# A transformer block with expert retrieval on one core: two more run-ahead chunks of the first expert product, issued earlier, and a reduction in place of four additions

## The chip, the core and the metric

The kernel runs on one core of a Trainium2 chip. The core has five engines with a queue each: PE (matrix products, into the PSUM memory), DVE and POOL (elementwise work), ACT (activations, copies, and here the evacuation of PSUM), and SP, which here only issues DMA transfers. Each queue is worked off in order: an instruction that waits holds up everything behind it on its engine. The metric is the device time of one execution in microseconds. Before the change it was 1732.71 us, the median of three executions (1732.04 to 1734.6).

## What is computed

Input and output are 512 tokens of 1024 numbers, float32. The first sub-layer mixes tokens (two kinds of attention, gates, an output projection, residual add). The change lies behind it, in the second sub-layer, a retrieval over 16384 single-neuron experts:

```python
q = (xb @ w_q).reshape(PEER_BLOCK, PEER_HEADS, 2, PEER_HALF)
scores = jnp.einsum('thpd,hpkd->thpk', q, sub_keys).astype(jnp.float32)
top_s, top_i = lax.top_k(scores, PEER_TOPK)
...
best_s, best_pos = lax.top_k(cand_s, PEER_TOPK)
expert = jnp.take_along_axis(cand_i, best_pos, axis=-1)
gate = jax.nn.softmax(best_s, axis=-1)
act = jax.nn.gelu(jnp.einsum('thkd,td->thk', u[expert], xb).astype(jnp.float32),
                  approximate=False)
return jnp.einsum('thk,thkd->td', (gate * act).astype(v.dtype), v[expert])
```

Each token has 8 heads with 16 experts each; an expert is a pair of keys (a, b), each of 128.

## The kernel before

The tokens are worked on in four tiles of 128. For one tile (GT, tile 0) the experts' rows of u and v are gathered by indirect DMA, and DVE forms dot products and weighted sums. For the other three (DT, 384 tokens) the kernel works densely: it computes u·x for all 16384 experts in 128 chunks of 128, applies Gelu, multiplies by a sparse matrix of gates, and multiplies by v.

*A chunk of the first product* is `first` (line 678): a 512 KB load of *ut* (two buffers, issued by SP); a split into a high part *uh* on ACT (line 673) and the remainder *ul* on POOL (line 674), in two halves with three buffers each; 24 matmuls into *pa* (lines 148 to 150, two PSUM buffers); and Gelu on ACT into *ga* (line 687), which has AHEAD buffers, so that chunks can run ahead.

*The decoding of the keys* is `retrieve` (line 638), once for each tile and each half of the key. ACT broadcasts the selector into a one-hot tile *oh* (line 646, two buffers), DVE compares it (line 647), multiplies it with the indices (line 649) and sums over the last axis of 16 (lines 651 to 653). The result is *ia* or *ib*. Behind the last tile's, DVE forms the row numbers *ex* (line 658), on which the gathers on POOL (line 762) wait. Between its steps `more(n)` issues chunks.

*The expansion* (lines 715 to 754): for each of the three dense tiles the keys are transposed on PE (line 718), copied by ACT (*sel*, line 720), and in eight blocks of 16 tokens DVE builds one-hots and weights (*o1*, *o2*, *ow*, lines 738 to 742: five ops of 2048 elements), PE multiplies them (*pg*, line 747, 32 matmuls), ACT evacuates the gates into *gres* (the first 8 chunks') and *stage*, and SP writes *stage* to *spool* in DRAM. One chunk is issued in each block, and behind the last block what AHEAD still lacks.

*The main loop* (line 799) has 128 iterations. Iteration i2 loads *vt*, splits it into *vh* (ACT) and *vl* (DVE), multiplies *ga* by *gres* (line 810) or by a slice of *gs*, read back from *spool* (line 813), splits that into *wh* and *wl*, issues chunk i2 + AHEAD, and accumulates 18 matmuls into *acc*. Behind each group of matmuls `tick` moves the gathered tile on by its pace (PACE): gathers on POOL, dot products (line 774) and weighted sums (line 784) on DVE.

What stands in an engine's queue is not the order of the text: a scheduler moves instructions of one engine past each other, so that chunks of the main loop appear among the expansion's blocks. The order of each queue is fixed when the kernel is built.

Of the kernel before, what the change touches and what calls it, by code (L numbers as in the profile page):

```python
# [15 lines left out]
OP = mybir.AluOpType  # L16
AX = mybir.AxisListType
# [13 lines left out]
OCT = 8  # L31
TB = 16
TI = 4
AHEAD = 37
S2, GAT, WB, UB, VB = 8, 4, 3, 3, 3
COLS = 3 * 3 * D
PACE = 1.05 * 2 * P * len(GT) / (COLS * (2 * P - AHEAD))

# [9 lines left out]
def block_kernel(ctx, tc, x, mix_gain, w_in, gate_bias, q_gain, k_gain, sinks, w_up_a, w_up_b, w_out,  # L48
                 ffn_gain, w_q, keys_t, peer_u, peer_v, peer_ut, out):
    nc = tc.nc  # L50
    V, A, G = nc.vector, nc.scalar, nc.gpsimd
# [93 lines left out]
    def mm3(ps, l, r, li, ri, start, stop):  # L145

        bg.tick(ps.shape[1] * 3)
        nc.tensor.matmul(ps, lhsT=l[0][li], rhs=r[0][ri], start=start, stop=False)  # L148
        nc.tensor.matmul(ps, lhsT=l[0][li], rhs=r[1][ri], start=False, stop=False)  # L149
        nc.tensor.matmul(ps, lhsT=l[1][li], rhs=r[0][ri], start=False, stop=stop)  # L150
# [487 lines left out]
    def retrieve(j):  # L638

        r = NT - 1 - j  # L640
        ia, ib = (gwk.tile([P, HEADS, 16], F32, name=f"{n}{j}") if j in DT else
                  rp.tile([P, HEADS, 16], F32, name=f"{n}{j}") for n in ("ia", "ib"))
        for sel, half, dst in ((a_, 0, ia), (b_, 1, ib)):
            oh = rp.tile([P, HEADS, 16, 16], BF16, name="oh", tag="oh", bufs=2)
            oh2 = oh.rearrange("p h k j -> p (h k) j")
            A.activation(oh2, sel[:, r, :, None].to_broadcast([P, P, 16]), AF.Copy)
            V.tensor_tensor(out=oh2, in0=oh2, in1=i16[:, None, :].to_broadcast([P, P, 16]), op=OP.is_equal)
            yield
            V.tensor_tensor(out=oh, in0=oh, in1=idf[:, r, :, half, None, :].to_broadcast([P, HEADS, 16, 16]), op=OP.mult)
            yield  # L650
            for n in (8, 4, 2):
                V.tensor_tensor(out=oh[:, :, :, 0:n], in0=oh[:, :, :, 0:n], in1=oh[:, :, :, n:2 * n], op=OP.add)  # L652
            V.tensor_tensor(out=dst, in0=oh[:, :, :, 0], in1=oh[:, :, :, 1], op=OP.add)
            yield
        KEYS[j] = ia, ib, gate[:, r]
        if j in GT:
            ROWS[j] = gwk.tile([P, HEADS, 16], I32, name=f"ex{j}")
            V.scalar_tensor_tensor(out=ROWS[j], in0=ib, scalar=128.0, in1=ia, op0=OP.mult, op1=OP.add)
# [19 lines left out]
    def first(i2):  # L678

        ut = us.tile([P, KD, P], F32, name="ut", tag="ut", bufs=2)  # L680
        nc.sync.dma_start(ut, peer_ut[i2])
        u = split(us, ut, "u", G, UB)
        pa = pa_.tile([P, 512], F32, name="pa", tag="pa")
        for k in range(KD):
            mm3(pa[:, :T], u[k // 4], h2T, (SL, k % 4, SL), (SL, k, slice(0, T)), k == 0, k == KD - 1)
        ga = upool.tile([P, T], F32, name="ga", tag="ga", bufs=AHEAD)
        A.activation(ga, pa[:, :T], AF.Gelu)  # L687
        return ga
# [3 lines left out]
    def more(n):  # L692
        for i2 in range(len(ahead), min(len(ahead) + n, AHEAD)):
            ahead[i2] = first(i2)

    more(2)
    for j in DT + GT:
        for i, _ in enumerate(retrieve(j)):
            if i % 3 == 0:
                more(1)  # L700
    ret.close()

# [1 line left out]
    with ExitStack() as st:  # L704
# [4 lines left out]
        oh = [P, TB // TI, P, TI]  # L709
# [5 lines left out]
        for j in DT:  # L715
# [15 lines left out]
            for tb in range(P // TB):  # L731
# [11 lines left out]
                for q in range(TB // TI):  # L743
                    pp = pg.tile([P, TI, P], F32, name="pg", tag="pg")
                    for i in range(TI):
                        for s in range(2):
# [7 lines left out]
                                  stage.rearrange("p (o i) t -> p o i t", i=OCT))  # L754
    more(AHEAD)

# [42 lines left out]
    for i2 in range(P):  # L799
# [15 lines left out]
        V.tensor_tensor(out=wl, in0=ga, in1=wh.bitcast(F32), op=OP.subtract)  # L815
        if i2 + AHEAD < P:
            ahead[i2 + AHEAD] = first(i2 + AHEAD)
        for b in range(2):
# [46 lines left out]
```

## Time and profile before

| | |
|---|---|
| median of 3 executions | 1732.71 us (1732.04 to 1734.6) |
| the profiled execution, its own time | 1733.96 us |
| its span, first to last instruction | 1732.2 us |
| PE busy | 1658.3 us (96%) |
| PE weight loads busy | 1470.5 us (85%) |
| DVE busy | 1329.1 us (77%) |
| POOL busy | 811.8 us (47%) |
| ACT busy | 746.2 us (43%) |
| DMA, mean | 209 GB/s |

The profile's picture of 40 slices, 43.3 us each, has a digit for each engine's busy tenths (9 is 90% or more) and one for the granted clock of TensorE. PE has a 9 in most slices; slices 13 and 14 (6 and 7, 520 to 606 us) are low, and in the first of them the clock row has its only digit under 9. This is the decoding of the keys; the expansion follows to about 801 us, then the main loop to the end. Elapsed time follows PE from 905 us on. A line of a timeline or of the chain gives the start in us, a duration in us, the engine, the line of code and the tiles written and read; "x8" merges eight instructions, and brackets hold the idle time in front and what ended it.

### The profile page before, as it was taken

The page shows a single profiled execution, that of the slowest core. Times are in us where ns is not written, and L with a number is a line of the kernel's source. Part 1 is how long each engine was busy: PE and PEld are TensorE (multiplying, and loading weights), DVE is VectorE, ACT ScalarE, POOL GpSimd, SP SyncE. Part 2 cuts the span into 40 slices and gives each one's busy share as a digit, 9 for nine tenths or more (in the row PEclk, how much of TensorE's full clock was granted, in tenths as well). Part 3 has the DMA queues.
Part 4 walks back from the last instruction along what each step waited for, and adds up shares of the span by engine and source line. Part 5 has one row for each costly group of instructions (what it writes and reads, how often), then busy time and mean ns, then how long its engine had stood idle before and what let it go on. Part 6 is the DMA issues. An engine that isn't in the chain of part 4 may idle for free.

```text
span 1732.2 us, 24914 instructions
## 1 busy us (share of the span) xinstructions
PE 1658.3 (96%) x8969; PEld 1470.5 (85%) x8969; DVE 1329.1 (77%) x2289; ACT 746.2 (43%) x1457; POOL 811.8 (47%) x628
## 2 busy tenths in 40 slices
PE   6999999999996799989899999999999999999998
PEld 5987777798885798989789999999999999998886
DVE  5444345736999998898999888898887878877874
ACT  4457635533324454545233443443343434343443
POOL 4100011512323644455567767776776666763310
PEclk9999999999998999999999999999999999999999
DMA  4321221133301365757998988989889888887874
GB/s 154 97 79 50 73 96 50 61 97 120 101 9 56 113 194 153 210 162 263 363 342 324 331 278 322 317 289 327 302 287 326 308 300 306 290 279 237 290 238 146
DMA packets 158347, 361.30 MB, mean 209 GB/s; under 512 B 10384, under 2 KB 86160, under 8 KB 156304
## 3 DMA queue, kind: packets, MB, share of 16 engines
q1 hardware_dynamic: 120496, 224.94, 38.7%
q0 software_dynamic: 36864, 134.23, 22.3%
q8 instruction: 70, 1.15, 0.3%
q10 hardware_dynamic: 864, 0.54, 0.1%
q14 instruction: 53, 0.43, 0.1%
HBM read 331.89 MB, written 27.26 MB: 207 GB/s over the span
## 4 chain that ended last, share of the span: by engine, by line
PE 78%; DVE 14%; issue 4%; POOL 2%; ACT 1%; DMA 1%; DVEq 0%; POOLq 0%; ACTq 0%
PE acc L148 10%; PE acc L150 10%; PE acc L149 10%; PE pa L150 8%; PE pa L148 8%; PE pa L149 8%; PE pg L747 5%; PE mm L149 5%; PE mm L150 5%; PE mm L148 5%; DVE tt L566 1%; PE z L462 1%; DVE oh L652 1%; PE mm L490 1%; DVE idx L568 1%
## 5 line engine op out<-in xcount | busy, mean ns | idle before, releaser
L674 POOL TENSOR_TENSOR ul<-ut,uh 128x512 fp32r<-128x512 f32 x256 | 388.4, 1519 | 183.4 <-ACT uh L673 172.7
L148 PE MATMUL pa<-h2Th,uh 128*128 128x384 f32 x1024 | 349.9, 342 | 16.8 <-ACT uh L673 16.4
L150 PE MATMUL pa<-h2Th,ul 128*128 128x384 f32 x1024 | 350.5, 342 | 9.0 <-POOL ul L674 9.0
L149 PE MATMUL pa<-h2Tl,uh 128*128 128x384 f32 x1024 | 348.8, 341 | 0.0
L149 PE MATMUL acc<-vl,wh 128*128 128x512 f32 x768 | 300.3, 391 | 4.6 <-DVE vl L674 4.6
L673 ACT ACTIVATE uh<-ut 128x512 fp32r<-128x512 f32 x256 | 160.8, 631 | 332.6 <-PE pa L149 234.3
L674 DVE TENSOR_TENSOR vl<-vt,vh 128x512 fp32r<-128x512 f32 x256 | 257.6, 1007 | 58.5 <-ACT vh L673 57.6
L148 PE MATMUL acc<-vh,wh 128*128 128x512 f32 x768 | 301.9, 393 | 0.0
L150 PE MATMUL acc<-vh,wl 128*128 128x512 f32 x768 | 300.7, 392 | 0.0
L762 POOL DMA_INDIRECT row<-peer_v,ex x128 | 157.5, 1231 | 162.9 <-DVE xg L784 120.4
L762 POOL DMA_INDIRECT row<-peer_u,ex x128 | 162.9, 1272 | 124.8 <-PE pa L150 51.2
L673 ACT ACTIVATE vh<-vt 128x512 fp32r<-128x512 f32 x256 | 159.8, 624 | 131.2 <-PE acc L150 128.9
L148 PEld LDWEIGHTS pa<-h2Th,uh 128*128 128x128 f32 x1024 | 196.1, 192 | 22.3 <-ACT uh L673 17.8
L150 PEld LDWEIGHTS pa<-h2Th,ul 128*128 128x128 f32 x1024 | 195.8, 191 | 11.9 <-POOL ul L674 11.9
L149 PEld LDWEIGHTS pa<-h2Tl,uh 128*128 128x128 f32 x1024 | 195.8, 191 | 3.7
L784 DVE SCALAR_TENSOR_TENSOR xg<-row,wt,xg 128x1024 f32<-128x1024 f32 x128 | 185.9, 1453 | 1.4 <-DMA row<-peer_v,ex 0.7
L774 DVE SCALAR_TENSOR_TENSOR row<-row,h 128x1024 f32<-128x1024 f32 x128 | 178.5, 1406 | 3.9 <-DMA row<-peer_u,ex 3.8
L149 PEld LDWEIGHTS acc<-vl,wh 128*128 128x128 f32 x768 | 144.7, 188 | 34.2 <-DVE vl L674 6.8
L150 PEld LDWEIGHTS acc<-vh,wl 128*128 128x128 f32 x768 | 144.6, 188 | 32.3
L148 PEld LDWEIGHTS acc<-vh,wh 128*128 128x128 f32 x768 | 144.5, 188 | 26.4
L158 DVE TENSOR_TENSOR wlo<-w,whi 128x1024 fp32r<-128x1024 f32 x52 | 65.0, 1251 | 87.1 <-ACT whi L157 82.9
L813 DVE TENSOR_TENSOR ga<-ga,gs 128x384 f32<-128x384 f32 x120 | 93.9, 798 | 44.3 <-ACT ga L687 44.3
(231 smaller groups left out, 2775.7 us busy)
## 6 DMA issues: line engine op xcount, KB each, us to landing
ut<-peer_ut SPq DMA_DIRECT2D x128, 512.0 KB
vt<-peer_v SPq DMA_DIRECT2D x128, 512.0 KB
spool<-stage SPq DMA_DIRECT2D x24, 960.0 KB
gs<-spool SPq DMA_DIRECT2D x15, 1536.0 KB
w<-w_in SPq DMA_DIRECT2D x17, 1024.0 KB
w<-w_q SPq DMA_DIRECT2D x8, 1024.0 KB
w<-w_out SPq DMA_DIRECT2D x4, 1024.0 KB
x<-x SPq DMA_DIRECT2D x4, 512.0 KB
```

Of the source, the lines that this page charges most:

```text
L148: nc.tensor.matmul(ps, lhsT=l[0][li], rhs=r[0][ri], start=start, stop=False)
L149: nc.tensor.matmul(ps, lhsT=l[0][li], rhs=r[1][ri], start=False, stop=False)
L150: nc.tensor.matmul(ps, lhsT=l[1][li], rhs=r[0][ri], start=False, stop=stop)
L158: eng.tensor_tensor(out=lo, in0=raw, in1=hi.bitcast(F32), op=OP.subtract))
L462: nc.tensor.matmul(z[:, :nk], lhsT=qT[:, h, cols(NT - 1 - j)], rhs=kbT[:, h // 2, row0(j):S], start=True, stop=True)
L673: A.activation(hi, src[:, 4 * b:4 * b + 4], AF.Copy)
L674: eng.tensor_tensor(out=lo, in0=src[:, 4 * b:4 * b + 4], in1=hi.bitcast(F32), op=OP.subtract)
L747: nc.tensor.matmul(pp[:, i, :], lhsT=o1[:, q, :, i], rhs=ow[:, s, q, :, i], start=(s == 0), stop=(s == 1))
L762: G.indirect_dma_start(out=t, out_offset=None, in_=src, in_offset=bass.IndirectOffsetOnAxis(ap=ex[:, h, k:k + 1], axis=0))
L774: V.scalar_tensor_tensor(out=t, in0=t, scalar=1.0, in1=h2, op0=OP.mult, op1=OP.mult, accum_out=wt[:, h, k:k + 1]))
L784: V.scalar_tensor_tensor(out=xj, in0=t, scalar=wt[:, h, k:k + 1], in1=xj, op0=OP.mult, op1=OP.add))
L813: V.tensor_tensor(out=g3, in0=g3, in1=gs[:, :, (i2 - RES) % OCT, :], op=OP.mult)
```

## The change

Three edits. AHEAD, the number of chunks that may run ahead of the main loop, goes from 37 to 39 (two more *ga* buffers, and PACE, which depends on it, rises by 219/217). In front of the decoding 8 chunks are issued instead of 2, and during it one at every second step instead of every third; a tile has 6 steps before and after, so 3 instead of 2. The text thus issues 8 + 12 = 20 chunks by the end of the decoding instead of 2 + 8 = 10; the expansion still issues one in a block, until AHEAD is reached. And each of the eight sums over 16 is one tensor_reduce, whose result is float32 as before, instead of additions of 8, 4, 2 and 1 pairs in 16-bit numbers. The lines behind the sum have numbers lower by 2 in the changed kernel.

```diff
-AHEAD = 37
+AHEAD = 39
...
-            for n in (8, 4, 2):
-                V.tensor_tensor(out=oh[:, :, :, 0:n], in0=oh[:, :, :, 0:n], in1=oh[:, :, :, n:2 * n], op=OP.add)
-            V.tensor_tensor(out=dst, in0=oh[:, :, :, 0], in1=oh[:, :, :, 1], op=OP.add)
+            V.tensor_reduce(out=dst, in_=oh, axis=AX.X, op=OP.add)
...
-    more(2)
+    more(8)
     for j in DT + GT:
         for i, _ in enumerate(retrieve(j)):
-            if i % 3 == 0:
+            if i % 2 == 0:
                 more(1)
```

How the queues change is seen at three places. The first is DVE's queue at the start of the decoding, for the first tile's two halves; *idf* holds the indices, *i* the numbers 0 to 15. Before:

```order
L647 TENSOR_TENSOR oh<-oh,i_3676 128x2048
L649 TENSOR_TENSOR oh<-oh,idf 128x2048
L652 TENSOR_TENSOR oh<-oh 128x128x8
L652 TENSOR_TENSOR oh<-oh 128x128x4
L647 TENSOR_TENSOR oh<-oh,i_3676 128x2048
L652 TENSOR_TENSOR oh<-oh 128x128x2
L649 TENSOR_TENSOR oh<-oh,idf 128x2048
L653 TENSOR_TENSOR ia_5144<-oh 128x128
```

In the changed kernel:

```order
L647 TENSOR_TENSOR oh<-oh,i_3676 128x2048
L649 TENSOR_TENSOR oh<-oh,idf 128x2048
L651 TENSOR_REDUCE ia_5366<-oh 128x128
L647 TENSOR_TENSOR oh<-oh,i_3676 128x2048
L649 TENSOR_TENSOR oh<-oh,idf 128x2048
L647 TENSOR_TENSOR oh<-oh,i_3676 128x2048
L651 TENSOR_REDUCE ib_5367<-oh 128x128
```

Each half has three DVE ops instead of six, and the third is the sum.

The second place is ACT's queue from the last one-hot broadcast of the decoding to the first evacuation of the expansion. Before:

```order
L646 ACTIVATE oh<-b__5053 128x2048
L673 ACTIVATE uh<-ut 128x512
L687 ACTIVATE ga<-pa 128x384
L673 ACTIVATE uh<-ut 128x512 x3
L687 ACTIVATE ga<-pa 128x384
L673 ACTIVATE uh<-ut 128x512
L720 ACTIVATE sel<-pg 128x256
L673 ACTIVATE uh<-ut 128x512 x2
L687 ACTIVATE ga<-pa 128x384
L673 ACTIVATE uh<-ut 128x512 x2
L687 ACTIVATE ga<-pa 128x384
L750 ACTIVATE gres<-pg 128x8x4
```

In the changed kernel:

```order
L646 ACTIVATE oh<-b__5053 128x2048
L671 ACTIVATE uh<-ut 128x512 x2
L685 ACTIVATE ga<-pa 128x384
...
L685 ACTIVATE ga<-pa 128x384
L718 ACTIVATE sel<-pg 128x256
L671 ACTIVATE uh<-ut 128x512 x2
L685 ACTIVATE ga<-pa 128x384
L671 ACTIVATE uh<-ut 128x512 x2
L685 ACTIVATE ga<-pa 128x384
L748 ACTIVATE gres<-pg 128x8x4
```

Between the last broadcast and *sel* stood two finished chunks (*ga*); now there are nine. On PE the key transposes stand behind chunk 19, and 22 chunks and three matmuls stand ahead of the first block's products; before there were 13 chunks and six matmuls.

The third place is PE's queue from the last block's products to the first accumulation (*acc*). Before, the rest of chunk 34 and the chunks 35, 36 and 37 stand between them:

```order
L747 MATMUL pg_7703<-ow_7664,o1_7662 128x128
L149 MATMUL pa_7764<-h2Tl_3170,uh_7760 128x384
...
L150 MATMUL pa_7902<-h2Th_3169,ul_7899 128x384
L148 MATMUL acc1_7871<-vh_7879,wh_7887 128x512
L149 MATMUL acc1_7871<-vl_7880,wh_7887 128x512
L150 MATMUL acc1_7871<-vh_7879,wl_7888 128x512
```

In the changed kernel:

```order
L745 MATMUL pg_7901<-ow_7862,o1_7860 128x128
L148 MATMUL pa_8105<-h2Th_3169,uh_8097 128x384
...
L148 MATMUL acc1_7921<-vh_7929,wh_7937 128x512
L148 MATMUL acc2_7922<-vh_7929,wh_7937 128x512
L148 MATMUL acc3_7923<-vh_7929,wh_7937 128x512
L149 MATMUL pa_8105<-h2Tl_3170,uh_8097 128x384
L150 MATMUL pa_8105<-h2Th_3169,ul_8098 128x384
L148 MATMUL pa_8105<-h2Th_3169,uh_8097 128x384
L149 MATMUL acc1_7921<-vl_7930,wh_7937 128x512
```

Here `pa_8105` is chunk 41, of which seven matmuls stand between the last block and the first accumulation; the chunks 39 and 40 stand among the first blocks of the third tile, and the last four blocks follow each other with no chunk between them.

## Rows read from the trace of the kernel before

**Rows 1.** Windows: us, busy us (instructions) of five engines, granted PE clock, DMA share, GB/s.

```profile
542.00:546.00 4.00, 3.54 (x12) 3.04 (x11) 3.93 (x6) 3.97 (x4) 0.00 (x0) 0.52 0.27 100
815.00:905.00 90.00, 83.68 (x406) 73.30 (x406) 87.74 (x117) 30.73 (x60) 57.53 (x45) 0.98 0.94 360
905.00:1600.00 695.00, 695.00 (x3506) 630.80 (x3505) 578.59 (x657) 277.36 (x508) 480.59 (x366) 1.00 0.87 301
```

**Rows 2.** Waits of PE, 505 to 610 us: total us, times, longest us.

```profile
PE pa L148 <- ACT uh L673: 16.4, 4, 10.2
PE pa L150 <- POOL ul L674: 7.3, 6, 1.5
PE pg L747 <- DVE o L742: 4.6, 1, 4.6
```

**Rows 3.** Timeline of PE: the fourth matmul of chunk 4.

```profile
545.63 0.46 PE L148 MATMUL pa<-h2Th,uh 128*128 128x384 f32 x1
```

**Rows 4.** Timelines of ACT and DVE at the start of the second token tile's expansion.

```profile
664.41 0.39 ACT L720 ACTIVATE sel<-pg 128x256 f16<-128x256 f32 x1
666.85 4.55 DVE L740 TENSOR_TENSOR ow<-o,part 128x2048 f16<-128x2048 f16 x2
679.16 1.22 DVE L741 TENSOR_TENSOR o<-rep,sel 128x2048 bf16<-128x2048 f16 x1
684.84 1.21 DVE L741 TENSOR_TENSOR o<-rep,sel 128x2048 bf16<-128x2048 f16 x1
```

**Rows 5.** Chain: products of each token tile's first block, and the last block.

```profile
608.00 3.96 PE pg L747 x32
...
677.02 3.96 PE pg L747 x32
...
746.69 3.93 PE pg L747 x32
...
797.64 3.82 PE pg L747 x32
```

**Rows 6.** Groups of DVE by form, 543 to 596 us: busy us, mean ns | idle.

```profile
L652 DVE TENSOR_TENSOR oh<-oh 128x1024 bf16<-128x1024 bf16 x8 | 9.8, 1223 | 0.0
...
L652 DVE TENSOR_TENSOR oh<-oh 128x512 bf16<-128x512 bf16 x8 | 6.9, 868 | 0.1
L652 DVE TENSOR_TENSOR oh<-oh 128x256 bf16<-128x256 bf16 x8 | 6.8, 849 | 0.0
L653 DVE TENSOR_TENSOR ia<-oh 128x128 f32<-128x128 bf16 x4 | 2.8, 704 | 0.0
```

**Rows 7.** Timeline of DVE and POOL beside two subtractions on POOL.

```profile
480.03 2.38 POOL L158 TENSOR_TENSOR wlo<-w,whi 128x1024 fp32r<-128x1024 f32 x1 [4.10 <-ACT whi L157]
...
480.97 0.29 DVE L567 MAX8 vals<-tt 128x8 f32<-128x128 f32 x1
...
486.53 2.39 POOL L158 TENSOR_TENSOR wlo<-w,whi 128x1024 fp32r<-128x1024 f32 x1 [4.12 <-ACT whi L157]
486.70 2.30 DVE L574 TENSOR_TENSOR cs<-vals 128x64 f32<-128x64 f32 x1
```

**Rows 8.** Groups of DVE by form, whole span: two reductions.

```profile
L193 DVE TENSOR_REDUCE qass<-s 128x8 f32<-128x512 f32 x4 | 2.7, 682 | 2.6 <-ACT s L191 2.6
...
L193 DVE TENSOR_REDUCE kass<-s 128x4 f32<-128x256 f32 x2 | 0.8, 415 | 0.4 <-ACT s L191 0.4
```

**Rows 9.** Chain: first matmuls of a chunk, an accumulation, the next chunk.

```profile
895.28 0.17 PE pa L148
...
899.45 0.24 PE acc L148
...
903.57 0.17 PE pa L148
```

**Rows 10.** Timelines of DVE and PE at the loop's entry.

```profile
801.72 7.14 DVE L810 TENSOR_TENSOR ga<-ga,gres 128x384 f32<-128x384 f32 x8 [5.39 <-ACT gres L750]
...
814.65 0.39 PE L148 MATMUL acc<-vh,wh 128*128 128x512 f32 x1
```

## The prediction

> **What bounds the kernel now.** I read the windows first. From 905 to 1600 us PE, the matmul engine, is busy in all 695 us [rows 1]: there every microsecond is PE's work, and the work is the same in both kernels (128 chunks of the first product, 128 accumulations, 24 blocks of expansion). So the change can only move the time in which PE stands still or runs at the low clock, all of it between 513 and 905 us. The list of waits gives the stills of the decoding stage: 10.2 us on ACT's *uh* (an Exp in ACT's queue waits for the top-16), 7.3 us on POOL's *ul*, 4.6 us on DVE's *o* [rows 2]. After the first of them PE ran at half clock (0.52) until 545.63, the fourth matmul of chunk 4 [rows 1, 3]. Then I read the chain: the first block of expansion starts on PE at 608.00, the first of the second and third token tile at 677.02 and 746.69, the last block at 797.64 [rows 5]. Last comes the loop's entry: first accumulation at 814.65 [rows 10].
>
> A chunk costs PE 899.45 − 895.28 = 4.17 us at full clock, an iteration's accumulation 903.57 − 899.45 = 4.12 [rows 9].
>
> **The decoding.** Before, PE has 13.25 chunks behind it when it starts to wait for block 1, at 608.0 − 4.6 = 603.4; the order of the change puts 22.125 chunks (22 and three matmuls) ahead of that place. Chunks 0 to 3 and the Exp stand as before, so the 10.2 us and the slow clock stay, and I start at 545.63 with 4.125 chunks in both. PE then needs 18.0 × 4.17 = 75.1 us: 620.7. To this I add 1 us for *uh* behind the one-hot broadcasts, 3 us where four *ul* stand behind the four row gathers on POOL (PE's waits for *ul* were 7.3/6 = 1.2 us each, 1.5 at most [rows 2]), and an estimated 2 us for chunk loads that share the DMA with those gathers: 626.7. The key transposes stand behind chunk 19, so 2.125 chunks (8.9 us) earlier: 617.8, and *sel* 0.6 later. From *sel* to the first product it took 677.02 − 664.41 = 12.6 us [rows 4, 5], DVE building the first one-hots: block 1 at 631.0, 23.0 us later than now, with 8.875 chunks (37.0 us) more done. **Lead: 14.0 us.**
>
> DVE's decoding then is not the bound. Before, the sums took 9.8 + 6.9 + 6.8 + 2.8 and another 2.7 for the second half's L653, 29.0 us busy for eight [rows 6]. The trace has no reduction of 2048. From 415 ns at 256 and 682 at 512 [rows 8] the slope is 1.04 ns an element: 682 + 1536 × 1.04 = 2.28 us, so 18.2 us for eight. The bounds: 4 × 682 = 2.73 us above; below, half of 2.28 if 16-bit data went at double rate, 1.14. I take 2.28, the straight line. Much of the 29 us was waiting: a two-input DVE op of 64 elements took 2.30 us, to the end of the POOL subtraction beside it, while the one-input MAX8 beside the same kind of subtraction took its 0.29 [rows 7]. In the expansion one *ul* costs DVE (4.55 − 2 × 1.14)/2 = 1.1 us [rows 4]. A reduction has one input, so a *ul* beside it should cost nothing; 16 two-input ops are left where there were 48. From 543 [rows 6] eight times two compares or products of 1.14 [rows 4] and a sum of 2.28 are 36.5 us, and if half of the sixteen *ul* there fall on two-input ops, 8 more: DVE ends near 588, just as PE comes to chunk 14 (545.6 + 9.9 × 4.17 + 1), where the first gather needs it. If each reduction is held once as well, that is 8.8 us more, of which ACT's ring of two one-hots would pass about half on to PE.
>
> On that point the Trainium skill states more than a row shows: SBUF — State Buffer, § Who interferes with whom, has it that tensor_reduce on trn2 never contends with GpSimd. By that rule the 8.8 us are out; no run here shows a reduction beside POOL.
>
> **The expansion.** Two token tiles repeat as they are, 746.69 − 608.00 = 138.7 us, plus 0.7 for the four matmuls that shift in: the third starts at 770.4. Here the order shows what the run-ahead does at its end: chunks 39 and 40 are still pulled in between the first blocks, then four blocks stand bare. DVE's clean block is 684.84 − 679.16 = 5.68 us [rows 4], and PE's 32 small products last 3.8 to 4.0 [rows 5]. So DVE sets the pace: 7 × 5.68 + 5 *ul* × 1.1 = 45.3, and the last block starts at 815.7, 18.1 after 797.64, with 41.0 chunks done by its end against 34.8 (25.9 us). **Lead: 7.8 us.** 6 us of PE's time went idle in the bare blocks.
>
> **The loop's entry.** Now three chunks (35.2 to 37, 13.4 us) cover DVE's multiplications by *gres*, 7.14 us for eight [rows 10] with *ul* beside them. In the change nothing covers them but seven matmuls of chunk 41. Without three *ul* of 1.1 the eight take an estimated 3.8; what DVE does behind them took 814.65 − 801.72 − 7.14 = 5.8 up to the accumulation, and I take 5.0, one *ul* fewer: 8.8 us after the last block's end at 815.7 + 3.8, so the first accumulation stands until 828.3. That is 13.7 after 814.65, and PE has 3.3 chunks (13.8 us) more done. **Lead: about nothing.** What the decoding gained is spent: it was chunks taken from a place where they covered DVE.
>
> **The first iterations.** From 814.65 to 899.45 nine iterations took 84.8 us instead of 9 × 8.29 = 74.6: 10.2 us lost, since DVE, busy 87.7 of 90 us [rows 1], multiplies 36 stored chunks by *gs* ahead of the *vl* that PE waits for. DVE's list up to the ninth iteration is nearly the same after, with six *ul* fewer beside it (some 13 for 19); the idle PE before it means that the iterations start earlier against DVE's list. I take 7 us lost: 3 gained.
>
> **The rest** is hidden or equal: 39 iterations without a chunk at the end for 37, no more PE work in sum; the pace of the gathers rises by 219/217, 0.9%, on a POOL that idles. Sum: 14.0 − 6.2 − 7.8 + 3 = 3 us less. The profiled execution took 1733.96 (span 1732.2 and 1.8 around it), so 1731; it lay 1.25 above the median of 1732.71, hence **1730** for a median.
>
> **The rivals.** *Faster: the decoding gives more than its price.* PE is not held by gathers, loads or broadcasts (6 us of mine), and the entry loses 5 us less, because DVE meets no *ul* there: 1730 − 11 = 1719. For it: the waits are sized by analogy, and PE without stills stays at the high clock. Against it: the gathers did delay *ul* before.
>
> *Slower: the bare entry.* The last block ends 18 to 22 us later than now. If DVE then needs from there as long to its ninth iteration as now, about 90 us, PE's lead of two chunks (8.3 us) is all that is given back, and the decoding's 14 us become a loss of 18.1 − 8.3 = 10; 1740. It decides from the point at which the last block ends over 11 us late and DVE, not PE, paces the nine iterations: PE's earlier chunks then don't matter. For it: DVE is busy 97% there, and the DMA engines 94% [rows 1]. PE idle for 8 us may also start at the low clock, as after the Exp; up to 4 us, mostly under DVE's time. Against it: fewer *ul*, and a load of *vt* that no longer stands behind one of *ut*.
>
> *The reduction is the slow way.* If a reduction takes the upper 2.73 us [rows 8], eight of them cost 3.6 us more than my line; DVE ends near 591, later than chunk 14, and all of it lands on the first gather and so on *ul* and PE: 1734. For it: no row has the size. Against it: two sizes on one line.
>
> VectorE: DVE Perf Modes in the Trainium skill, § Rules for kernel authors, speaks for this rival: it says to expect tensor_reduce at the single rate, as the slowest DVE op, and the table above that has 16-bit tensor_tensor at twice the rate. From that page's cycle formula I estimate 2.30 us for the reduction and 1.72 for four additions, 4.6 us in eight against the change, were DVE the bound; by that rule alone it would come to 1735. The trace agrees on the single rate (1.04 ns an element) and not on the additions, which took 3.6 us beside POOL.
>
> That the change does not do what it says is excluded by the order.
>
> **How the numbers follow.** Netting out, 0.45, with a range of its own of 1723 to 1737; faster 0.22; slower 0.25; slow reduction 0.08. This kernel's measurement can tell 0.2%, 3.5 us, from nothing. Faster than 1729.2: 0.20 of the first and all of the second, 0.42. Within: 0.20 of the first, 0.05 of the last, 0.03 of the third, 0.28. Slower: the rest, 0.30. The range reaches to both rivals with their bounds: 1714 to 1746.
>
> **What would show it.** In the profile after: no PE wait of 1 us or more between 546 and 590; block 1 on PE at 627 to 635 (right within 4 us); block starts in the last half of the third tile some 5.7 us apart, PE waiting on *o*; a still of PE of 6 to 9 us before the first accumulation; reductions of 2.2 to 2.4 us, none near 3.4. Wrong, if block 1 comes before 622, or if accumulation nine lies more than 90 us behind the last block.

## The result: 0.73% slower, and the profile after

The changed kernel takes 1745.12 us, the median of four executions (1744.34 to 1745.39); the kernel before took 1732.38 beside it. The ratio is 1.0073, with a 95% interval of 1.0061 to 1.0084: slower by 12.7 us where 3 less were forecast. The profiled execution took 1745.39 (span 1743.7, against 1732.2).

I read the windows first, as in [rows 1]. A line gives the stretch, its length, then busy us (instructions) of PE, PE's weight loads, DVE, ACT and POOL, the granted clock, the DMA share and GB/s.

```profile
543.00:592.00 49.00, 46.77 (x248) 44.11 (x248) 48.46 (x27) 28.44 (x38) 33.98 (x21) 0.96 0.35 113
592.00:622.00 30.00, 27.54 (x150) 25.26 (x150) 0.00 (x0) 10.48 (x21) 20.92 (x18) 1.00 0.54 177
...
826.00:834.00 8.00, 5.38 (x15) 4.55 (x16) 7.33 (x15) 2.65 (x5) 3.92 (x3) 0.51 0.91 302
831.00:919.00 88.00, 75.69 (x348) 65.74 (x349) 78.58 (x114) 28.03 (x54) 46.49 (x37) 0.95 0.92 344
920.00:1600.00 680.00, 679.96 (x3430) 616.75 (x3429) 567.11 (x650) 271.08 (x498) 478.70 (x360) 1.00 0.87 304
```

From 920 us on PE is full, as it was from 905 on. The second line is the one to stop at: for 30 us DVE does nothing at all. Its timeline (start, duration, what, and in brackets the idle time in front and what ended it) says what it waited for; the answer to it before is that DVE went from the decoding (end 596) straight to the first one-hots.

```profile
588.16 2.29 DVE L651 TENSOR_REDUCE ib<-oh 128x128 f32<-128x2048 bf16 x1
590.48 1.36 DVE L656 SCALAR_TENSOR_TENSOR ex<-ib,ia 128x128 int32<-128x128 f32 x1
...
622.30 0.29 DVE L723 TENSOR_SCALAR two<-pg 128x128 int32<-128x128 int32 x1 [30.46 <-ACT sel L718]
```

DVE is done with the decoding at 591.8. *sel* comes when PE has done the key transposes behind chunk 19 (from 620.9), and ACT the evacuation: 622.3. The blocks of [rows 5] start 26.6, 27.4, 27.1 and, the last one, 21.5 us later. In the chain:

```profile
634.62 3.96 PE pg L745 x32
...
704.40 3.96 PE pg L745 x32
...
773.78 3.94 PE pg L745 x32
...
819.09 3.96 PE pg L745 x32
```

The loop's entry on PE, which answers to [rows 10]: the bare blocks wait for DVE, then PE stands 5.15 us for ACT's *ga*, and the first accumulation comes at 831.23, 16.6 later than before.

```profile
808.75 3.96 PE L745 MATMUL pg<-ow,o 128*128 128x128 f16 x32 [2.71 <-DVE o L740]
814.43 3.94 PE L745 MATMUL pg<-ow,o 128*128 128x128 f16 x32 [1.72 <-DVE o L740]
819.09 3.95 PE L745 MATMUL pg<-ow,o 128*128 128x128 f16 x32 [0.73 <-ACT stage L749]
828.19 0.69 PE L148 MATMUL pa<-h2Th,uh 128*128 128x384 f32 x1 [5.15 <-ACT ga L685]
...
831.23 1.65 PE L148 MATMUL acc<-vh,wh 128*128 128x512 f32 x3 [0.43 <-ACT vh L671]
```

Between the first accumulation (number 0) and number 9 PE then waits for DVE. In the list of waits of 800 to 920 us (total us, times, longest) *vl* has 12.1 us; before it had 4.6 in three waits.

```profile
PE acc L149 <- DVE vl L672: 12.1, 6, 3.5
PE pa L148 <- ACT ga L685: 5.1, 1, 5.1
```

A piece of DVE's and one of PE's timeline show how such a wait comes about: seven multiplications by *gs* for later iterations, 6.20 us, stand ahead of the *vl* of this one, and PE waits 2.91 us for it.

```profile
896.52 6.20 DVE L811 TENSOR_TENSOR ga<-ga,gs 128x384 f32<-128x384 f32 x7
902.64 0.68 DVE L672 TENSOR_TENSOR vl<-vt,vh 128x512 fp32r<-128x512 f32 x1
```

```profile
903.38 0.50 PE L149 MATMUL acc<-vl,wh 128*128 128x512 f32 x1 [2.91 <-DVE vl L672]
```

Accumulation 9 starts at 918.8, 19.5 later than before's 899.3. With two chunks fewer left behind it, 824.9 us remain instead of 832.9, so the span grows by 19.5 − 8.0 = 11.5.

### The profile page after: what moved, and what is told of

Same layout as the page of the kernel before. It is cut to its first block, busy times and chain, and to the rows that moved or that the text cites. A ratio compares the mean times of both kernels' runs of the same rounds, so it can differ in the third digit from the quotient of the medians.

```text
span 1743.7 us, 24888 instructions
## 1 busy us (share of the span) xinstructions
PE 1661.8 (95%) x8969; PEld 1470.6 (84%) x8969; DVE 1306.5 (75%) x2265; ACT 746.5 (43%) x1457; POOL 817.8 (47%) x628
## 4 chain that ended last, share of the span: by engine, by line
PE 81%; DVE 8%; issue 6%; POOL 2%; DMA 2%; ACT 1%; DVEq 0%; POOLq 0%; ACTq 0%
PE acc L148 9%; PE acc L150 9%; PE acc L149 9%; PE pa L150 8%; PE pa L149 8%; PE pa L148 8%; PE mm L150 6%; PE mm L149 6%; PE mm L148 6%; PE pg L745 4%; DVE ga L811 1%; POOL ul L672 1%; DVE ow L738 1%; PE z L462 1%; PE mm L490 1%
## 5 line engine op out<-in xcount | busy, mean ns | idle before, releaser
L149 PE MATMUL acc<-vl,wh 128*128 128x512 f32 x768 | 300.6, 391 | 12.1 <-DVE vl L672 12.1
L672 DVE TENSOR_TENSOR vl<-vt,vh 128x512 fp32r<-128x512 f32 x256 | 252.3, 986 | 59.4 <-ACT vh L671 58.7
L760 POOL DMA_INDIRECT row<-peer_v,ex x128 | 163.8, 1280 | 156.6 <-DVE xg L782 112.9
L782 DVE SCALAR_TENSOR_TENSOR xg<-row,wt,xg 128x1024 f32<-128x1024 f32 x128 | 181.6, 1419 | 2.6 <-DMA row<-peer_v,ex 1.9
L772 DVE SCALAR_TENSOR_TENSOR row<-row,h 128x1024 f32<-128x1024 f32 x128 | 173.6, 1370 | 9.5 <-DMA row<-peer_u,ex 9.5
L812 ACT ACTIVATE wh<-ga 128x384 fp32r<-128x384 f32 x128 | 67.1, 524 | 140.8 <-PE acc L149 140.7
```

What stands on the lines that cost most here:

```text
L672: eng.tensor_tensor(out=lo, in0=src[:, 4 * b:4 * b + 4], in1=hi.bitcast(F32), op=OP.subtract)
L760: G.indirect_dma_start(out=t, out_offset=None, in_=src, in_offset=bass.IndirectOffsetOnAxis(ap=ex[:, h, k:k + 1], axis=0))
L772: V.scalar_tensor_tensor(out=t, in0=t, scalar=1.0, in1=h2, op0=OP.mult, op1=OP.mult, accum_out=wt[:, h, k:k + 1]))
L782: V.scalar_tensor_tensor(out=xj, in0=t, scalar=wt[:, h, k:k + 1], in1=xj, op0=OP.mult, op1=OP.add))
L812: A.activation(wh, ga, AF.Copy)
```

## Experiments

All times are medians beside runs of the kernel before on the same chip (1731.8 to 1733.4). The "ninth accumulation" of the expectations is number 9, counted from 0. The table gives, in us from the profiled run's start, block 1's first product, accumulations 0 and 9 on PE, and DVE's waits for *sel* in all (two or three waits). These places are those of one execution, which lies within 2.4 us of its run's median, but for e6, e8 and e10 (5 to 6 us above) and e7 and e13 (4.4 and 6.2 below). "Pinned" means that the scheduler may not move the multiplications by *gs* and the subtractions *wl*; "spread", that the multiplications by *gs* are given out evenly over the iterations.

| run | block 1 | *sel* waits | acc 0 | acc 9 | median | ratio, 95% |
|---|---|---|---|---|---|---|
| before | 608.0 | 12.8 | 814.7 | 899.3 | 1732.4 | |
| after | 634.6 | 43.8 | 831.2 | 918.8 | 1745.1 | 1.0061 to 1.0084 |
| e1 reduction alone | 598.4 | 13.2 | 803.6 | 889.4 | 1724.0 | 0.9934 to 0.9961 |
| e2 after, additions | 644.9 | 47.1 | 841.9 | 929.9 | 1757.6 | 1.0131 to 1.0162 |
| e3 before, AHEAD 39 | 608.0 | 12.7 | 826.9 | 907.0 | 1732.8 | 0.9990 to 1.0008 |
| e4 after, AHEAD 37 | 633.2 | 42.9 | 826.6 | 911.3 | 1746.0 | 1.0065 to 1.0092 |
| e5 after, every third step | 617.1 | 27.6 | 825.0 | 912.5 | 1739.8 | 1.0024 to 1.0051 |
| e6 after, all pinned | 633.8 | 45.4 | 831.2 | 903.2 | 1774.1 | 1.0219 to 1.0252 |
| e7 e1, all pinned | 595.9 | 12.3 | 800.0 | 875.5 | 1750.6 | 1.0094 to 1.0123 |
| e8 e1, keys early | 597.0 | 5.5 | 802.8 | 884.8 | 1714.4 | 0.9882 to 0.9914 |
| e9 after, 24 pinned | 634.1 | 43.4 | 830.7 | 902.8 | 1755.8 | 1.0112 to 1.0141 |
| e10 e8, 24 pinned | 598.7 | 5.6 | 804.5 | 879.1 | 1728.8 | 0.9959 to 0.9988 |
| e11 e10, Exp later | 618.1 | 20.9 | 812.1 | 887.1 | 1742.4 | 1.0043 to 1.0068 |
| e12 after, spread | 633.7 | 43.9 | 831.3 | 903.6 | 1737.2 | 1.0018 to 1.0044 |
| e13 e8, spread | 593.9 | 1.1 | 792.2 | 867.0 | 1707.8 | 0.9852 to 0.9888 |
| e14 after, more(2) | 611.6 | 24.9 | 819.4 | 904.3 | 1728.9 | 0.9972 to 0.9993 |

**The parts of the change: e1 to e5 and e14.** e1 is before with the reduction alone, e2 the changed kernel without it; e3 and e4 set AHEAD alone (`37` to `39` in before, `39` to `37` in after).

> The kernel before with the one edit of tensor_reduce for the four additions; AHEAD 37, 2 chunks ahead of the decoding, one at every third step. Theory D (from the first block of expansion to the ninth accumulation the time is DVE's, 284 to 291 us in both profiles, so the time follows the start of block 1, less 4.15 us for each chunk more that AHEAD allows): DVE ends the decoding some 6 us earlier (590 instead of 596), block 1 starts at 601 to 604 instead of 608.0, the ninth accumulation moves with it, and the time is 1726 to 1730. Theory R (the reduction is what costs: its 2.28 us are slower than the additions once these are not held): block 1 not before 608, 1733 to 1738.

> The changed kernel with the four additions put back, AHEAD 39 and the earlier chunks kept. Theory D: DVE idles 30 us between the decoding and the first one-hots of the expansion there, so the reduction's few us are hidden for the most part: block 1 at 633 to 640, time 1744 to 1751, slower than before as with the reduction. Theory R: without the reduction the loss is gone, 1730 to 1735.

> The kernel before with AHEAD 39 alone (and PACE, which follows from it). The two chunks more stand behind the last block, ahead of the first accumulation. Theory D: block 1 and the last block stay at 608 and 798, the ninth accumulation comes at 899 to 903 (DVE has its list to do in any case, and PE's cover for it is 8.3 us longer), and with two chunks fewer left behind it the time is 1725 to 1729. Theory A (more run-ahead costs by itself, through two more multiplications by gs that DVE does early and through a faster pace of the gathers): the ninth accumulation at 908 or later, 1733 or more.

> The changed kernel with AHEAD back at 37. Theory D: block 1 stays at 634 to 635, the ninth accumulation at 916 to 919, and two chunks more are left behind it: 1750 to 1754, the slowest of the four. Theory A: with 37 the loss shrinks, 1735 to 1742.

The reduction is a gain, theory R is out: 8.8 us alone, 12.5 within the change (1757.6 − 1745.1). Both gains are larger than theory D had them: e1 is under its 1726 to 1730, and e2, where the reduction was to be hidden, is over its 1744 to 1751. In e2 PE waits 6.6 us in three waits for *uh* behind the Exp's, in the change not at all; in ACT's queue *uh* stands behind the one-hot broadcasts, which wait 16.1 us for DVE's sums, 7.1 in the change. In e1 DVE ends the decoding at 588.1 instead of 596.0 and goes on without a stop: PE's last key transposes stand behind 10 chunks (574.9), and *sel* is done at 586.8. DVE's timeline of e1:

```profile
585.46 2.29 DVE L651 TENSOR_REDUCE ib<-oh 128x128 f32<-128x2048 bf16 x1
587.78 0.29 DVE L656 SCALAR_TENSOR_TENSOR ex<-ib,ia 128x128 int32<-128x128 f32 x1
588.08 0.29 DVE L723 TENSOR_SCALAR two<-pg 128x128 int32<-128x128 int32 x1
```

AHEAD 39 is worth nothing in either kernel. Theory A all but has e3 (1733 or more, measured 1732.8) and fails in e4; theory D fails in both: accumulation 9 comes 7.7 us later in e3 and 7.5 earlier in e4, just what the two chunks left behind it give and take. So the change is −8.8 (reduction), 0 (AHEAD), and the earlier chunks: 1745.1 − 1724.0 = 21.1.

e5 and e14 undo the halves of the earlier chunks; 18.1 and 16.1 chunks stand ahead of block 1, 14.3 in e1 and 22.1 in the change.

```diff
-            if i % 2 == 0:        # e5
+            if i % 3 == 0:
...
-    more(8)                       # e14
+    more(2)
```

> The changed kernel with a chunk at every third step of the decoding again (8 chunks ahead of it, the reduction and AHEAD 39 stay). On PE 18.1 chunks instead of 22.1 stand ahead of block 1, only the last block is bare instead of four. Theory I (what the change loses is DVE's idle time of 30 us, in which the key transposes stand behind the chunks on PE): block 1 at 616 to 620, half of the way back to the kernel with the reduction alone (1724), 1731 to 1738. Theory P (the loss lies in the chunks that are missing at the end, the four bare blocks and the bare entry): with these covered the loss goes whole, 1722 to 1728.

> The changed kernel with 2 chunks ahead of the decoding again (every second step, the reduction and AHEAD 39 stay). 16.1 chunks stand ahead of block 1, and the first tile's key transposes behind chunk 4. Theory I (only chunks behind which DVE idles cost): DVE idles under 5 us behind the decoding, block 1 at 602 to 606, 1723 to 1728. Theory L (each chunk ahead of block 1 costs the same, by the line through 14.3 chunks and 1724 and 18.1 chunks and 1740): 1730 to 1734.

The loss shrinks with the chunks ahead of block 1. The ends (bare blocks, entry) are nearly covered in e5, and it still loses, so theory P is out. With AHEAD's 8.0 taken off, accumulation 9 stands at 889.4, 896.3, 904.5 and 910.8 for 14.3, 16.1, 18.1 and 22.1 chunks: 3.8 and 4.1 us for each chunk at first, 1.6 for each of the last four. The times of e14 (1728.9, between the two theories) and e5 (1739.8, over theory I's 1738) say the same: theory I had the direction, and not the size, and theory L's straight line doesn't hold either. DVE's first wait for *sel* is 11.4 us even in e14 (under 5 forecast), 13.8 in e5, 30.5 in the change. The expectation of e14 has the key transposes behind chunk 4; that is so of the first alone (546.8). The other two stand behind 14 chunks, 5.5 us after DVE's end at 587.9, and then *sel* stands in ACT's queue behind the *uh* of more chunks, which wait for their loads. Timelines of PE and of ACT in e14:

```profile
593.41 0.27 PE L716 MATMUL pg<-ident,ib 128*128 128x128 f32 x1
...
589.82 0.63 ACT L671 ACTIVATE uh<-ut 128x512 fp32r<-128x512 f32 x1 [2.61 <-DMA ut<-peer_ut]
...
597.98 0.63 ACT L671 ACTIVATE uh<-ut 128x512 fp32r<-128x512 f32 x1 [6.63 <-DMA ut<-peer_ut]
...
598.89 0.38 ACT L718 ACTIVATE sel<-pg 128x256 f16<-128x256 f32 x1
```

**DVE's idle time at the change of tiles: e8.** The transposes, *sel* and what hangs on it are made for the next tile ahead of the fifth block of this one (`decode(j)` holds lines 714 to 728):

```diff
+        nxt = decode(DT[0])
         for j in DT:
+            sel, part, power = nxt
             for tb in range(P // TB):
+                if tb == 4 and j != DT[-1]:
+                    nxt = decode(DT[DT.index(j) + 1])
```

> The kernel before with the reduction, and with the key transposes and sel of the second and third token tile put ahead of the fifth block of the tile before (sel, part and power with two buffers), so that DVE doesn't idle 6.2 and 7.0 us at the change of tiles. Theory I (DVE's idle time between the decoding and the ninth accumulation is what the time follows): the last block starts 9 to 13 us earlier than 791.3, and the time is 1713 to 1718. Theory P (PE's chunks between the blocks set the pace, and what is gained in front is lost at the loop's entry): 1721 to 1726.

The time is as theory I has it: the waits for *sel* fall from 13.2 to 5.5, and 9.6 us are gained against e1. The last block starts at 781.4 instead of 789.0, 7.6 us earlier and not 9 to 13 (the 791.3 of the expectation was read too late by 2.3). The profiled execution, 5.0 us above the median, has a stall that no theory had (below); what it costs the others isn't shown.

**The entry: e6, e7, e9, e10, e12, e13.** e6 and e7 keep the multiplications by *gs* and *wl* in program order; e9 and e10 do so for the first 24 iterations:

```diff
-            V.tensor_tensor(out=g3, in0=g3, in1=gs[:, :, (i2 - RES) % OCT, :], op=OP.mult)
+            tc.keep_in_program_order(
+                V.tensor_tensor(out=g3, in0=g3, in1=gs[:, :, (i2 - RES) % OCT, :], op=OP.mult))
...
-        V.tensor_tensor(out=wl, in0=ga, in1=wh.bitcast(F32), op=OP.subtract)
+        tc.keep_in_program_order(V.tensor_tensor(out=wl, in0=ga, in1=wh.bitcast(F32), op=OP.subtract))
```

> The changed kernel with the multiplications by gs (L811) and the subtractions wl kept in program order, so that DVE does one in each iteration instead of bursts of two to seven ahead of the vl for which PE waits. Theory H (in the first iterations PE waits for vl because of these bursts): from the first to the ninth accumulation 70 to 76 us instead of 87.6, and the time is 1729 to 1735. Theory G (PE waits there because DVE's dot products wait for gathers, with the DMA engines 92% busy): the ninth accumulation stays at 915 to 920, 1742 to 1747.

> The kernel before with the reduction, and with the same pinning of the multiplications by gs and of wl. From the first accumulation to the ninth it is 85.8 us without the pinning, PE's own work is 74.6. Theory H: 75 to 79 us, and 1714 to 1718. Theory G: no change, 1722 to 1726.

> The changed kernel with the multiplications by gs and wl in program order in the first 24 iterations alone; behind them the queue is free again. The pinning in all iterations cut the first nine to 72.0 us, and lost 44 us later, where iterations have no chunk to cover DVE. Theory H (bursts in the first iterations are the loop entry's loss): 71 to 74 us from the first to the ninth accumulation, the rest as in the changed kernel, 1727 to 1733. Theory S (the bursts are only put off, and what DVE multiplies ahead in the 24 iterations is missing later): 1738 to 1746.

> The kernel before with the reduction, the key transposes put ahead of the fifth block of the tile before, and the pinning in the first 24 iterations. Without the pinning: first accumulation 802.8, ninth 884.8, median 1714.4. Theory H: 74 to 77 us between the two instead of 82.0, time 1705 to 1710. Theory S: 1713 to 1717.

In front theory H is right in all four: accumulation 0 to 9 takes 72.0 (e6), 75.5 (e7), 72.2 (e9) and 74.6 us (e10), instead of 87.6, 85.8, 87.6 and 82.0. The gathers were not the bound: in e6 DVE still waits 6.5 us for gathered rows there, and PE 0.6 for DVE. But every one of them is slower in the end, by 20.7 to 49.4 us behind accumulation 9: the bursts do work that is needed later. In e7 an iteration without a chunk takes 4.9 to 5.6 us instead of 4.08, as PE waits for *wh* in each of the last 37; waits of PE from 1548 to 1740 us:

```profile
PE acc L148 <- ACT wh L813: 23.6, 37, 1.2
```

Pinned for 24 iterations, the bursts come behind them, in e9 from 905 to 1100 us:

```profile
PE acc L148 <- ACT wh L817: 6.1, 3, 2.4
PE acc L150 <- DVE wl L818: 5.8, 4, 1.8
```

So theory S, and worse: e9 and e10 end 9.8 and 11.8 us over its ranges. It left open whether there is a place at all, and e12 and e13 give the multiplications out one and a half to an iteration:

```diff
+        while gi < P and (gi <= i2 or gi - RES < (i2 - 8) * 3 // 2) and (gi <= i2 or gi in ahead):
...
+            tc.keep_in_program_order(
+                V.tensor_tensor(out=g3, in0=g3, in1=gs[:, :, (gi - RES) % OCT, :], op=OP.mult))
+            gi += 1
```

> The changed kernel with the multiplications by gs given out evenly: from the eighth iteration on three in two iterations, in program order with the dot products, instead of bursts in the first nine. As many are done ahead before the last 37 iterations begin. Theory H (the place of the bursts is the loop entry's loss): 71 to 75 us from the first to the ninth accumulation, no loss behind it, 1728 to 1734. Theory S (DVE has no room for them elsewhere): the loss comes back behind the ninth accumulation, 1739 to 1750.

> The kernel before with the reduction and the key transposes put ahead (1714.4), and the multiplications by gs given out evenly as in e12. Theory H: 75 to 77 us from the first to the ninth accumulation instead of 82.0, and 1706 to 1710. Theory S: 1713 to 1725.

There is. e12 takes 72.3 us to accumulation 9, and 8 us of the 15 stay (1737.2 against 1745.1); the rest goes behind it to waits for *ul* and *vl*, so it lies between the theories. e13 gains 6.6 us on e8 by the medians, where 7.2 went out of the entry. (The profiled executions differ in front of it too: e13's has no such stall as e8's, and its first accumulation comes 10.6 us earlier.) It is the fastest of all, 24.2 us (1.3%) under the kernel before. PE is full from accumulation 0 on; windows of its profiled execution (1701.6, the lowest of five), with the columns as above:

```profile
543.00:792.00 249.00, 237.60 (x1583) 226.86 (x1582) 242.67 (x178) 132.03 (x308) 131.74 (x76) 0.99 0.61 184
792.00:867.00 75.00, 75.00 (x382) 68.11 (x381) 53.75 (x69) 27.73 (x54) 50.26 (x39) 1.00 0.87 318
```

**A miss: e11.** It puts the gates' Exp behind the *uh* of five chunks.

> As e10, with 5 chunks ahead of the decoding instead of 2 and the Exp of the gates behind their uh in ACT's queue, so that PE doesn't stand still for 10.2 us at 528 us and does some 2.4 chunks there; 15.2 chunks instead of 14.3 stand ahead of block 1. Theory I (from the decoding to the ninth accumulation the time is DVE's): block 1 within 2 us of e10's, and the chunks that PE has done save at most 2 us each behind it: 1702 to 1708 if e10 is at 1707. Theory E (PE is the bound once DVE's idle times are gone): 10 us and the low clock behind the stall come back whole, 12 us less than e10.

Both theories fail: 13.7 us slower than e10. The order of the queues put *sel* late again: PE's transpose of the gates stands behind 13 chunks (601.0), and *sel* (605.4) behind the *uh* of more. DVE waited 17.6 us for it, and block 1 came 19.4 us later. It is the fault of the change once more, not a test of the Exp's stall; that stall stays untested.

## Why the prediction was wrong

- *The reduction* was right: 2.28 us forecast, eight took 2.27 to 2.29. The groups of DVE by form, 543 to 600 us, answer to [rows 6]: 18.2 us for 29.0.

```profile
L651 DVE TENSOR_REDUCE ia<-oh 128x128 f32<-128x2048 bf16 x4 | 9.1, 2286 | 0.1
L651 DVE TENSOR_REDUCE ib<-oh 128x128 f32<-128x2048 bf16 x4 | 9.1, 2276 | 0.0
```

The rival of the slow reduction is out. The Trainium skill's VectorE: DVE Perf Modes, § Rules for kernel authors, has tensor_reduce at the single rate, as the slowest DVE op. Its rate is that of the trace, but e1 gains: four additions took 3.6 us in the mean. DVE's timeline before has four without a *ul* beside them, in 2.1 us, and an addition of 1024 beside one (POOL, from 571.28), which alone takes 1.75.

```profile
552.77 1.68 DVE L652 TENSOR_TENSOR oh<-oh 128x1024 bf16<-128x1024 bf16 x3
554.49 0.42 DVE L653 TENSOR_TENSOR ib<-oh 128x128 f32<-128x128 bf16 x1
...
572.08 1.75 DVE L652 TENSOR_TENSOR oh<-oh 128x1024 bf16<-128x1024 bf16 x1
```

- *The decoding* was near: block 1 at 634.6 for 631.0. DVE ended the decoding at 591.8 for 588; PE's waits for *ul* took 4.7 us in seven, where 3 were taken.
- *The expansion* was right in length (45.3 us from the third tile's start to the last block, as forecast), in part by luck: PE has no wait from 773.8 to 806, so the first three distances of the blocks, 8.2, 7.3 and 7.5 us, are PE's chunks and products, and not DVE's pace as forecast. The last block is 3.4 us late, as block 1 was late.
- *The loop's entry* was right too: 12.1 us from the last block to the first accumulation, 12.6 forecast, though PE's still is 5.15 us and not 6 to 9.
- *The first iterations* are the step that failed. I took 7 us lost, "since the idle PE before it means that the iterations start earlier against DVE's list". PE's own work from accumulation 0 to 9 is 9 × 4.12 + 7.7 × 4.17 = 69.2 us; it took 87.6, so 18.4 were lost, 11.4 more than I took. With the 3.4 of the blocks and −0.5 at the entry, that is the error but for 0.2: forecast −3, measured +11.5. Of the 18.4, 12.1 are PE's waits for *vl*; in the other 6.3 PE is busy for longer than at full clock (granted 0.95 in the stretch, 0.98 before). DVE's list did not shrink (114 instructions, 110 before), and DVE had not got further in it: where PE idled, DVE idled too (4.3 us for *gres*, 5.4 before, then 7.0 for gathered rows, 0.9 before). e6, e9 and e12 show that the bursts are the loss: with them moved out of the stretch, it is 2.8 to 3.1 us.

```profile
DVE two L723 <- ACT sel L718: 43.8, 3, 30.5
DVE row L772 <- DMA row<-peer_u,ex: 7.0, 5, 2.2
DVE ga L808 <- ACT gres L748: 4.3, 1, 4.3
```

These are DVE's longest waits from 540 to 920 us. Behind this step stands one of method: I kept a ledger of PE's lead, chunk by chunk, and asked where DVE ends the decoding, but not what it does next. The 30.5 us it waits for *sel* lie in the prediction's own times (588 to 618.4), and no term prices them. DVE's account from the end of its decoding to accumulation 9, before and in the changed kernel (windows, columns as above):

```profile
596.04:899.28 303.24, 281.98 (x1781) 266.22 (x1780) 281.50 (x262) 136.58 (x332) 158.32 (x98) 0.96 0.72 237
591.84:918.80 326.96, 286.69 (x1777) 267.92 (x1778) 267.98 (x263) 137.74 (x333) 160.74 (x98) 0.93 0.67 219
```

DVE ends the decoding 4.2 us earlier and is busy 13.5 us less, but it idles 59.0 us instead of 21.7: together the 19.5 us by which accumulation 9 is late. In e1, e14, e5 and the change its idle time is 26.6, 37.7, 44.0 and 59.0 us, in the order of their times, and e8, with the waits for *sel* at the change of tiles cut, is faster than e1. That the early chunks cost the time is shown by e1, e5 and e14. That they cost it through the wait for *sel* is argued from this order; the sizes don't follow the wait alone, and no run keeps the early chunks and brings *sel* early.

- *The rival "the bare entry"* came true by its own condition. The last block was over 11 us late (21.5), and accumulation 9 lay 99.7 us behind it, 101.6 before (the rival's "about 90" was misread, its sum doesn't use it). Its 1740 lacks the 3.4 us of the blocks; I gave it 0.25. The prediction's own sign of being wrong, more than 90 us there, came.

Not settled is why AHEAD's two chunks cost in front exactly what they save behind. Two more multiplications and four more *ul* fall into the same stretch, in which DVE is busy 6.4 us longer in e3 than before, and 6.1 longer in the change than in e4; no run separates them.

## What to carry to other kernels

When work is moved ahead on one engine, ask which other engine is kept from its next task meanwhile: follow the late operand (*sel* here) through the queues in which more work now stands in front of it (PE's and ACT's). A lead in chunks counts only where the engine that has it is the one that waits for nobody. And work done early by an engine is not waste because it delays something; look for a place with room, rather than forbid it.

## What the hardware showed that was not expected

One subtraction of *ul* on POOL, 1.3 us when undisturbed, took 12.98 us in e8, to 1.1 us behind the end of a stretch (630.8 to 649.0) in which DVE's two-input ops followed each other without a gap; PE then waited 5.34 us for it, and DVE 7.30 for PE. Timelines of POOL, and of DVE:

```profile
637.17 12.98 POOL L672 TENSOR_TENSOR ul<-ut,uh 128x512 fp32r<-128x512 f32 x1 [6.46 <-ACT uh L671]
```

```profile
647.81 1.21 DVE L743 TENSOR_TENSOR o<-rep,sel 128x2048 f16<-128x2048 f16 x1
656.32 1.23 DVE L746 TENSOR_TENSOR o<-rep,sel 128x2048 bf16<-128x2048 f16 x1 [7.30 <-PE pg L752]
```

So here it is POOL that is held, where [rows 7] show DVE held. It is not the only case: e10 has one of 12.93 us, the kernel before two of 5.5 and 5.7, e13 none over 2.4. A reduction and a *ul* leave each other alone. SBUF — State Buffer, § Who interferes with whom, in the Trainium skill has it that tensor_reduce never contends with GpSimd (POOL) on trn2; the trace agrees. Timelines in the changed kernel:

```profile
548.01 2.29 DVE L651 TENSOR_REDUCE ia<-oh 128x128 f32<-128x2048 bf16 x1
548.46 1.29 POOL L672 TENSOR_TENSOR ul<-ut,uh 128x512 fp32r<-128x512 f32 x1 [1.56 <-ACT uh L671]
```

And the granted clock fell to its lower level (1.2 of 2.4 GHz) among the bare blocks, behind a still of PE of 2.7 us, and stayed there through the entry, with stills of 0.7 to 5.2 us; before, it was 1.00 from 800 to 834 us. The prediction had it as a possibility. A window of the changed kernel:

```profile
810.00:833.80 23.80, 15.77 (x101) 14.14 (x100) 18.83 (x27) 11.47 (x31) 3.92 (x3) 0.50 0.69 213
```
